# Plain copies of the weight-sum units on SyncE's queue, and units that begin at even and odd tiles in turn

## The chip, the core and the metric

The kernel runs on one core of a Trainium2 chip. The core has a matrix engine (PE, with its weight loads shown as PEld), a vector engine (DVE), a scalar engine (ACT), GpSimd (POOL) and SyncE (SP). Each engine works through its own instruction queue in order and waits for the others through semaphores. SP here only issues DMAs; POOL issues DMAs and also computes. The metric is the device time of one execution in microseconds, median over several runs; lower is better.

## What is computed

One transformer layer over 1024 tokens of width 1024. The part that matters here is the gated MLP:

```python
hn = rmsnorm(h, norm_ffn_g[i])
up = hn @ w_up[i]                       # 1024 x 5632
gt, val = up[..., :D_FF], up[..., D_FF:]
gt = causal_dwconv(gt, conv_w[i], conv_b[i])
h = h + (jax.nn.gelu(gt, approximate=False) * val) @ w_down[i]
```

Before it stand a pooling mixer and chunked attention with their projections, behind it a gated embedding and a last norm. D_FF is 2816.

## The kernel before

All matrix products are made in single precision from two halves of each number: every `mm3` is three matmuls (lines 130 to 132) of a high and a low part, and `split` (lines 134 to 136) makes the two parts, the high one on ACT (line 135) and the low one on DVE (line 136).

**The first projection** (called up here) goes over 22 tiles `fi` of 128 gate and 128 value columns. Each tile is a two by two block product made by seven products in place of eight, with sums and differences of the blocks (a scheme of Strassen's kind). A product is 12 matmuls, so a tile is 84. The order of the products in a tile is 1, 5, 2, 6, 3, 7, 4 (`steps`, line 710). Products 5, 6, 3 and 7 need sums of weight quarters. For tiles 3 to 21 POOL makes them (`summed`, line 758, the instruction of line 759) from quarters that SP loads (line 755) into a ring of buffers in the tiles F and X. What the products give is read out of PSUM by DVE and ACT: after product 6, DVE adds into `u2` (line 858), and product 7, which writes on into the same PSUM bank, cannot begin until DVE has done that. At the end of a tile come the convolution and the GELU (lines 869 to 882), the product of gate and value (lines 885 and 886) and the store of the tile to DRAM, `GD[fi]` (line 921, on SP).

**The second projection** (down) multiplies by `w_down`, with the same seven products over 11 pairs of tiles. Its weight sums are not made by POOL but by DMAs, ahead of time, in a DRAM array `SD`. There are 14 such units `u`: 0 to 2 belong to the first three tiles of up, 3 to 13 to `w_down`. `weight_sums(u, part)` (line 548) issues one of six parts. The even parts are plain copies (part 0: two copies of weights into `SD`; parts 2 and 4: one copy from `SD` to `SD` each). The odd parts are DMAs that add weights to what lies in `SD` (part 1: two of them; parts 3 and 5: one each). Every part reads what the part before it wrote. All of these transfers move 256 KB and are issued by POOL (line 556). Units 0 to 7 run during attention. Units 8 to 13 run during up, and only these are changed: 24 copies and 24 adding transfers.

In `up` (line 905) the units from 8 on are due by the tile's number: unit 8 + z begins at tile 5 + 2z and issues one part a tile, so that an odd tile issues only even parts (plain copies) and an even tile only odd parts (adding ones). Before them POOL does a small copy from the tile's GELU output (line 919), which ties the issue to that moment; `keep_in_program_order` pins an instruction behind the one traced before it on its engine.

**What sets the order.** PE's order is written out by hand. For the other engines a scheduler orders the instructions at build time by its own clock: an instruction that is not pinned can be moved ahead of others traced before it. The store of line 921 is not pinned, and loads of later tiles may go ahead of it. The launch sets a size for the scratch of dynamic DMAs (line 1261: `dynamic_dma_scratch_size=1024`).

## Time and profile before

| | us |
|---|---|
| median of 3 runs (lowest, highest) | 1145.69 (1145.26, 1145.73) |
| profiled execution, its own time | 1144.89 |
| its span, first to last instruction | 1143.1 |
| PE busy | 1124.2 |
| DVE busy | 887.3 |
| ACT busy | 577.8 |
| POOL busy | 292.1 |

The profile holds one execution. "Busy" is the time in which an engine has an instruction running. Matmuls overlap in the pipeline, so that a busy PE is not one at its peak. A row of the timeline has the start in us, the duration, the engine, the line of the kernel, the operation, what it writes and reads, and, where the engine stood idle before it, how long and which instruction seems to have released it. A row marked x3 merges three instructions. SPq rows are the issues on SP's queue. Stores of the tiles of up begin at 411.7 us (tile 0) and end at 812.8 us (tile 21).

### The profile page before, as it was taken

To read this page: it belongs to the slowest core of one execution; us is meant where nothing else is said; L and a number is where in the kernel's file an instruction comes from. 1 tells how busy PE (TensorE), PEld (TensorE's weight loads), DVE (VectorE), ACT (ScalarE), POOL (GpSimd) and SP (SyncE) were. 2 spreads that over 40 slices of the span, in tenths; PEclk is the share of its full clock that TensorE was granted. 3 is DMA by queue.
4 is the path that set the end of the run, shared out by engine and by line. 5 is a ranking of instruction groups with operands and counts; after the bars stand their busy time and mean duration, and the time that the engine had idled before them with its cause. 6 is when DMAs were issued, how large, how long until landed. Compare 5 with 4: busy or idle time off the path is not lost.

```text
span 1143.1 us, 15305 instructions
## 1 busy us (share of the span) xinstructions
PE 1124.2 (98%) x5517; PEld 945.0 (83%) x5517; DVE 887.3 (78%) x1371; ACT 577.8 (51%) x1001; POOL 292.1 (26%) x323
## 2 busy tenths in 40 slices
PE   8999999999999999999999999999999999999996
PEld 7988998888888878888887878788888888888886
DVE  7678878878756788989898888888896789757344
ACT  8568677765554543443433434343444557445222
POOL 0012324275002213445454645443000000000000
PEclk9999999999999999999999999999999999999998
DMA  7134656543500343133536463414683555310012
GB/s 265 38 86 113 160 122 172 120 90 131 185 10 19 120 158 100 65 120 92 147 104 173 97 171 101 102 37 127 229 280 98 169 186 176 108 48 1 1 74 75
DMA packets 62572, 133.46 MB, mean 117 GB/s; under 512 B 7392, under 2 KB 9696, under 8 KB 62048
## 3 DMA queue, kind: packets, MB, share of 16 engines
q1 hardware_dynamic: 49552, 100.96, 26.6%
q0 software_dynamic: 11200, 29.37, 12.9%
q10 hardware_dynamic: 1744, 2.17, 0.5%
q8 instruction: 43, 0.70, 0.3%
q14 instruction: 33, 0.27, 0.1%
HBM read 116.73 MB, written 45.09 MB: 142 GB/s over the span
## 4 chain that ended last, share of the span: by engine, by line
PE 84%; DVE 7%; ACT 3%; issue 3%; DMA 1%; POOL 1%; SPq 0%; DVEq 0%; POOLq 0%; ACTq 0%
PE PS L130 26%; PE PS L132 26%; PE PS L131 26%; PE PS L370 2%; DVE R L136 1%; PE PS L388 1%; ACT F L356 1%; PE PS L387 1%; DVE B L378 1%; POOL X L759 1%; DMA GD<-X 1%; DMA F<-in_w_qk 1%; DVE F L346 1%; DVE X L886 0%; PE PS L345 0%
## 5 line engine op out<-in xcount | busy, mean ns | idle before, releaser
L130 PE MATMUL PS<-R,R 128*128 128x512 f32 (+1 forms) x932 | 360.3, 387 | 5.9 <-DVE F L858 4.6
L132 PE MATMUL PS<-R,R 128*128 128x512 f32 (+1 forms) x932 | 356.3, 382 | 0.0
L131 PE MATMUL PS<-R,R 128*128 128x512 f32 x868 | 338.3, 390 | 0.4 <-DVE R L231 0.3
L130 PEld LDWEIGHTS PS<-R,R 128*128 128x128 f32 x932 | 175.5, 188 | 40.5 <-ACT R L135 7.0
L132 PEld LDWEIGHTS PS<-R,R 128*128 128x128 f32 x932 | 175.3, 188 | 34.4 <-DVE R L136 0.2
L131 PEld LDWEIGHTS PS<-R,R 128*128 128x128 f32 x868 | 163.5, 188 | 32.7 <-DVE R L231 1.4
L132 PE MATMUL PS<-B 128*128 128x512 f32 x316 | 123.1, 390 | 0.1
L130 PE MATMUL PS<-B 128*128 128x512 f32 x316 | 123.2, 390 | 0.0
L131 PE MATMUL PS<-B 128*128 128x512 f32 x316 | 123.0, 389 | 0.0
L136 DVE TENSOR_TENSOR R<-F,R 128x512 fp32r<-128x512 f32 (+1 forms) x117 | 93.9, 814 | 17.7 <-ACT R L135 17.3
L759 POOL TENSOR_TENSOR X<-X 128x512 f32<-128x512 f32 x42 | 77.3, 1840 | 116.5 <-DVE R L136 58.5
L135 ACT ACTIVATE R<-X 128x512 fp32r<-128x512 f32 x97 | 60.3, 629 | 88.2 <-PE PS L131 52.5
L136 DVE TENSOR_TENSOR R<-X,R 128x512 fp32r<-128x512 f32 x97 | 94.5, 975 | 12.2 <-ACT R L135 12.2
L135 ACT ACTIVATE R<-F 128x512 fp32r<-128x512 f32 (+1 forms) x121 | 71.9, 612 | 62.8 <-PE PS L131 26.3
L135 ACT ACTIVATE B<-F 128x512 fp32r<-128x512 f32 (+1 forms) x94 | 60.7, 647 | 78.2 <-PE PS L131 59.3
L659 POOL TENSOR_TENSOR small<-small 128x4 f32<-128x4 f32 (+1 forms) x7 | 8.1, 1161 | 336.2 <-DVE small L658 336.2
L136 DVE TENSOR_TENSOR B<-F,B 128x512 fp32r<-128x512 f32 (+1 forms) x94 | 66.4, 710 | 30.1 <-ACT B L135 30.0
L132 PEld LDWEIGHTS PS<-B 128*128 128x128 f32 x316 | 59.3, 188 | 12.9 <-DVE B L136 0.6
L131 PEld LDWEIGHTS PS<-B 128*128 128x128 f32 x316 | 59.3, 188 | 12.4
L130 PEld LDWEIGHTS PS<-B 128*128 128x128 f32 x316 | 59.3, 188 | 12.2
L131 PE MATMUL PS<-B,R 128*128 128x256 f32 (+1 forms) x208 | 64.0, 308 | 0.0
L356 ACT ACTIVATE F<-F,small 128x640 f32<-128x640 f32 (+2 forms) x64 | 44.4, 693 | 23.2 <-DVE small L354 15.7
(178 smaller groups left out, 2097.0 us busy)
## 6 DMA issues: line engine op xcount, KB each, us to landing
SD<-in_w_down POOLq DMA_DIRECT2D x66, 256.0 KB, 5.3
X<-in_w_up SPq DMA_DIRECT2D x53, 256.0 KB, 3.2
F<-SD SPq DMA_DIRECT2D x49, 256.0 KB, 2.7
R<-GD SPq DMA_DIRECT2D x44, 256.0 KB, 5.4
F<-in_w_down SPq DMA_DIRECT2D x33, 256.0 KB, 3.6
F<-in_w_up SPq DMA_DIRECT2D x32, 256.0 KB, 3.0
SD<-SD POOLq DMA_DIRECT2D x28, 256.0 KB, 3.8
GD<-X SPq DMA_DIRECT2D x11, 512.0 KB, 4.3
```

Source lines behind the costliest of these rows:

```text
L130: pe.matmul(ps, ahi, bhi, start=first, stop=False, skip_group_check=more)
L131: pe.matmul(ps, ahi, blo, start=False, stop=False, skip_group_check=more)
L132: pe.matmul(ps, alo, bhi, start=False, stop=last, skip_group_check=more)
L135: act.activation(hi, src, AF.Copy)
L136: dve.tensor_tensor(lo, src, rv(hi), ALU.subtract)
L346: dve.tensor_tensor_reduce(S.rearrange("p (a b) -> p a b", a=2), PS[:, 4:6, 0:320], b.rearrange("p (a b) -> p a b", a=2), 1.0, BIG, ALU.ad ...
L356: act.activation(S[:, 0:n], S[:, 0:n], AF.Exp, bias=s_[:, 0:1], scale=-1.0, accum_out=s_[:, 1:2])
L370: pe.transpose(pst[:, j * P:(j + 1) * P], S[:, j * P:(j + 1) * P], ident)
L378: dve.tensor_tensor(lo, pst, rv(hi), ALU.subtract)
L387: pe.matmul(O, V[:, k, h], pt[:, 0, idx], start=n_ == 0, stop=False)
L388: pe.matmul(O, V[:, k, h], pt[:, 1, idx], start=False, stop=n_ == len(ks) - 1)
L759: pool.tensor_tensor(rawu[to], rawu[a], rawu[b], op)
```

## The change

In `weight_sums` the engine that issues a plain copy becomes a parameter; its default is POOL, so that the units of the attention stage are as before. In `up` the plain copies go to SP, pinned behind the store of the tile, which itself is now pinned behind what was traced before it on SP. Adding transfers stay on POOL. A unit 8 + z now begins at tile 4 + 2z + (z mod 2): at tiles 4, 7, 8, 11, 12 and 15 where they were 5, 7, 9, 11, 13 and 15. So a tile now issues parts of both kinds. POOL's small copy of line 919 stands only in tiles where an adding part is due.

```diff
-        def weight_sums(u, part):
+        def weight_sums(u, part, copies=pool):
...
-                tc.keep_in_program_order(pool.dma_start(to, src, **({"accum_op": op} if op else {})))
+                tc.keep_in_program_order(pool.dma_start(to, src, accum_op=op) if op else copies.dma_start(to, src))
...
-            due = [(u, fi - 5 - 2 * (u - EARLY)) for u in range(EARLY, NK + UP_SUMS)
-                   if 0 <= fi - 5 - 2 * (u - EARLY) < 6]
-            if due:
+            due = [(EARLY + z, fi - 4 - 2 * z - z % 2) for z in range(NK + UP_SUMS - EARLY)]
+            due = [(u, part) for u, part in due if 0 <= part < 6]
+            if any(part % 2 for _, part in due):
                 tc.keep_in_program_order(pool.tensor_copy(small[:, 78:79], y[:, 0:1]))
             values_in(y)
-            sp.dma_start(GD[fi], y)
+            tc.keep_in_program_order(sp.dma_start(GD[fi], y))
             for u, part in due:
-                weight_sums(u, part)
+                weight_sums(u, part, sp)
```

## The prediction

> **What bounds the kernel now.** I read the page, then the waits of PE, then the stretch in which the changed transfers run, tile by tile, by the timelines of SP, POOL and DVE.

> ```profile
> span 1143.1 us, 15305 instructions
> PE 1124.2 (98%) x5517; PEld 945.0 (83%) x5517; DVE 887.3 (78%) x1371; ACT 577.8 (51%) x1001; POOL 292.1 (26%) x323
> ```

> PE is busy nearly all the time, so only gaps of PE can be won. The waits of PE between 480 and 830 us, where units 8 to 13 run, are one row:

> ```profile
> PE PS L130 <- DVE F L858: 3.8, 4, 1.2
> ```

> Four waits, all of product 7 for DVE's line 858. The same view on four short windows finds one each behind tiles 10, 14, 16 and 20; the row of the first (604 to 608 us):

> ```profile
> PE PS L130 <- DVE F L858: 1.0, 1, 1.0
> ```

> What they cost the whole is better read from the stores of the tiles (SP's timeline, with two rows of loads that I need below):

> ```profile
> 562.37 0.33 SPq L921 DMA_DIRECT2D GD<-X  x1
> ...
> 601.43 0.33 SPq L921 DMA_DIRECT2D GD<-X  x1
> ...
> 718.49 0.33 SPq L755 DMA_DIRECT2D F<-in_w_up  x1
> 737.07 0.33 SPq L921 DMA_DIRECT2D GD<-F  x1
> 756.11 0.33 SPq L921 DMA_DIRECT2D GD<-X  x1
> ...
> 778.04 1.53 SPq L755 DMA_DIRECT2D F<-in_w_up  x2
> ```

> Tile 17 is stored at 737.07, tile 18 at 756.11: an undisturbed tile takes 19.04 us. From tile 8 (562.37) to tile 17 there are nine: 171.36 us. They took 174.70. The excess, 3.34 us, holds the first three waits (behind tiles 10, 14 and 16) with the restart of PE after each. The fourth is behind tile 20.

> Now POOL around the store of tile 8 and of tile 10, and the held issues of tiles 12, 14 and 16:

> ```profile
> 558.61 2.54 POOL L556 DMA_DIRECT2D SD<-in_w_down  x3
> 561.36 2.15 POOL L759 TENSOR_TENSOR X<-X 128x512 f32<-128x512 f32 x1 [0.21 <-DVE R L136]
> ...
> 597.66 2.58 POOL L556 DMA_DIRECT2D SD<-in_w_down  x3
> 602.62 0.81 POOL L556 DMA_DIRECT2D SD<-in_w_down  x1 [2.38 <-DVE F L870]
> 603.17 1.57 POOL L759 TENSOR_TENSOR X<-X 128x512 f32<-128x512 f32 x1
> ...
> 636.02 2.57 POOL L556 DMA_DIRECT2D SD<-in_w_down  x3
> 640.72 0.81 POOL L556 DMA_DIRECT2D SD<-in_w_down  x1 [2.13 <-DVE R L136]
> ...
> 674.10 2.57 POOL L556 DMA_DIRECT2D SD<-in_w_down  x3
> 679.73 0.81 POOL L556 DMA_DIRECT2D SD<-in_w_down  x1 [3.06 <-DVE F L870]
> ...
> 714.12 2.54 POOL L556 DMA_DIRECT2D SD<-in_w_down  x3
> 718.93 0.81 POOL L556 DMA_DIRECT2D SD<-in_w_down  x1 [2.26 <-DVE R L136]
> ```

> Tile 8 issues three adding transfers, and the weight sum behind them (line 759, for product 7) runs at 561.36, 1.01 us ahead of the store. Tile 10 issues four. The first three go out, the fourth stands 2.38 us, and the sum comes at 603.17, 1.74 us behind the store: 2.75 us late. What held the fourth? The landing of the first of each group, from its own row (issues at 597.66, 636.02, 674.10, 714.12):

> ```profile
> DMA to landing us min/median/max: 4.6/4.6/4.6
> DMA to landing us min/median/max: 4.4/4.4/4.4
> DMA to landing us min/median/max: 5.3/5.3/5.3
> DMA to landing us min/median/max: 4.5/4.5/4.5
> ```

> The firsts land at 602.3, 640.4, 679.4 and 718.6. The fourths go at 602.62, 640.72, 679.73 and 718.93: 0.3 us behind the landing, four times of four. So three of these transfers fit in flight and the fourth waits for a place. The DVE instructions that the profile names ended at that moment by chance.

> The late sum then holds ACT, DVE and PE. DVE's rows of tiles 8 and 10:

> ```profile
> 565.17 0.68 DVE L858 TENSOR_TENSOR F<-PS,F 128x512 f32<-128x512 f32 x1
> ...
> 605.44 0.69 DVE L136 TENSOR_TENSOR R<-X,R 128x512 fp32r<-128x512 f32 x1 [2.83 <-ACT R L135]
> 606.05 0.68 DVE L858 TENSOR_TENSOR F<-PS,F 128x512 f32<-128x512 f32 x1
> ```

> DVE takes its queue in order: the split that needs the late sum (605.44) stands ahead of line 858. Undisturbed, line 858 ends 3.48 us behind the store (565.85 against 562.37); in tile 10 it ended 5.30 behind (606.73), and PE had waited 1.0 us, so it was wanted at 605.7. An undisturbed one would have ended at 601.43 + 3.48 = 604.9, with 0.8 us to spare. That is the small end of the slack, since tile 10's store was itself late: 39.06 us behind tile 8's, where two tiles are 38.08.

> **The change, part by part.** *The most adding transfers in one tile.* Before, tiles 10, 12, 14 and 16 have four each (parts 5 and 3 of one unit each and the two of part 1). With starts at 4, 7, 8, 11, 12, 15, the 24 adding transfers fall on tiles 5, 7 to 18 and 20, as 2, 1, 2, 3, 1, 1, 3, 3, 1, 1, 3, 1, 1 and 1. No tile has four; tiles 9, 12, 13 and 16 have three. Three is tile 8's case: all issued by 561.15, the sum not delayed, PE not waiting. So the holds go and the 3.34 us with them. Tiles 9 and 13 have their three at odd tiles, where only copies stood; no row shows three adding ones there, and tile 8's is the nearest.

> *What POOL no longer issues:* 24 copies. Tile 11 has four, of which these are the last two, with the sum behind them:

> ```profile
> 619.07 1.06 POOL L556 DMA_DIRECT2D SD<-in_w_down  x2
> 620.79 2.13 POOL L759 TENSOR_TENSOR F<-F 128x512 f32<-128x512 f32 x1 [0.66 <-DVE R L136]
> ```

> 0.53 us each, 12.7 us in all. POOL then stood 0.66 us for DVE, so the copies were covered and their removal is worth nothing. The two copies of line 919 that fall away (14 tiles in place of 16) are worth nothing for the same reason. [...]

> *What SP now issues:* up to three copies behind a store (tiles 8, 11, 12, 15). SP's issues take 0.33 us; at the 0.53 of POOL's as the upper bound three are 1.0 to 1.6 us. I take 0.33, the row of the same queue. Queued behind are the loads of line 755, which now wait for the pinned store and the copies. But between 718.49 and 778.04 SP issued no load of line 755 while three tiles ran: the loads are some three tiles ahead, and a few microseconds cost a product nothing. A copy waits for an adding transfer issued a tile earlier; the rows above show landings within 5.3 us, about a quarter of a tile, so there is no wait. An adding transfer in turn waits for copies issued behind the store before it, some 15 us earlier (19.04 less the 3.76 by which 558.61 stands ahead of tile 8's store).

> *The cover that could fail.* POOL makes product 5's sums ahead, as soon as a load lands:

> ```profile
> 569.43 1.46 POOL L759 TENSOR_TENSOR X<-X 128x512 f32<-128x512 f32 x1 [5.93 <-DMA X<-in_w_up]
> 573.13 3.97 POOL L759 TENSOR_TENSOR X<-X 128x512 f32<-128x512 f32 x2 [2.24 <-DVE R L136]
> ```

> This sum isn't urgent, but it stands in POOL's queue ahead of those of products 6 and 3. Between its end (570.89) and theirs (573.13) POOL has 2.24 us. Copies in front of the loads delay the landing: at 0.5 us each (the spacing of the issues in tile 11) by 1.5, at twice that by 3.1. Up to 2.24 us is free; the upper end pushes the urgent sums by 0.9, which just about uses up the 0.8 of slack. I take 0.1 us in all, nearest to the lower end, with 0 and 1 kept for the range. What a shifted sum does to DVE in tiles that go well I put at 0, with half a microsecond either way; in that lies the longest wait, 1.2 us behind tile 20, which has one adding transfer before and after.

> *The sum*, on the profiled execution's own 1144.89 (span 1143.1 and 1.8 around it): 1144.89 - 3.34 + 0.1 = 1141.65. The median of the runs lies 0.80 above that execution, so 1142.4. About 0.2% (2.3 us) is what a measurement of this kernel can tell from no change; 3.2 us is 0.28%.

> **Rivals.** *The holds stay (1145.7).* If a fourth transfer is held not for a place but by what DVE does at that moment, as the profile's releasers say, three in a tile are held too: four heavy tiles before, four after, and the 3.34 us stay. For it: the named releasers. Against it: tile 8's three and the 0.3 us. [...]

> *Half is given back (1144).* The sums made ahead shift by a microsecond or two and slow DVE in tiles that now go well, or the scheduler, whose clock sees other POOL and SP times, orders DVE less well. Two stalls of the size of those here (3.34 / 3 = 1.1 us) give 1142.4 + 2.2 = 1144.6; one gives 1143.5. I write 1144.

> *Slower (1148).* The loads fall so far behind the copies that the sum made ahead stands in the way of products 6 and 3 in every tile with three copies or three adding transfers: tiles 8, 9, 11, 12, 13, 15 and 16. It decides from a landing 3.0 us later than now (2.24 of room and 0.8 of slack). At 4.2 us later each tile loses 1.2: 7 x 1.2 = 8.4, and 1142.4 + 8.4 = 1150.8; with only the four tiles of three copies hit, 1147.2. I write 1148, between. Against it: it needs more than 1.4 us per copy, where tile 11's, issued 0.53 us apart, left the sum of line 759 on time.

> **Chances.** The forecast 0.62, the holds stay 0.12, half given back 0.17, slower 0.09. The forecast lies beyond 0.2% on the fast side, the two middle cases are within 0.2% (above 1143.4), the last is beyond it on the slow side: 0.62, 0.29, 0.09. The range goes from the forecast less 0.5 us and the spread of the runs (1.0 in all, 1141.4; I take 1141.2, since tile 20's wait may shrink too) up to the holds that stay, with the spread: 1146.2.

> **What would show it.** Right: no POOL row of line 556 with idle time of 2 us before it between 480 and 800 us; the sum behind the adding transfers about 1.0 us ahead of the store in every tile; PE's waits for line 858 down from four to one; stores of tiles 8 and 17 some 171.4 us apart; the loads of line 755 still ending around 718. Wrong: a held second or third adding transfer; PE waiting for another line of DVE; the sums of products 6 and 3 released by a load or by line 759 in the tiles with three copies; a longer wait behind tile 20.

## The result, and the profile after

| | before | after |
|---|---|---|
| runs of the first comparison: median (lowest to highest), us | 1145.47 (1143.16 to 1147.90) | 1139.30 (1138.51 to 1141.21) |
| profiled execution, us | 1144.89 | 1138.89 |
| its span, us | 1143.1 | 1137.1 |

The ratio after to before is 0.9953, with a 95% interval of 0.9938 to 0.9967. The change saved 6.2 us in this comparison where 3.2 were forecast, and the time lies below the low end of the range (1141.2). In all the comparisons of this study together the kernel before ran 77 times (one more run, at 4017 us, is left out): from 1141.93 to 1148.05, median 1144.72. The kernel after ran 17 times: median 1139.32, and fourteen of them lie between 1138.51 and 1139.66. By these the change is worth 5.4 us.

The page of the kernel after, the two rows shown of before:

```profile
span 1137.1 us, 15326 instructions
PE 1121.7 (99%) x5517; PEld 944.6 (83%) x5517; DVE 891.4 (78%) x1371; ACT 577.9 (51%) x1001; POOL 281.5 (25%) x297
```

PE has the same 5517 matmuls. Its busy time fell from 1124.2 to 1121.7, which idle time alone cannot do: some matmuls of before ran slower. This comes back below. The waits of PE between 475 and 825 us, one row as before (in total, times, longest):

```profile
PE PS L130 <- ACT R L135: 1.4, 1, 1.4
```

Of the four waits for line 858 none is left. The one wait that remains is behind tile 20, as before, now for ACT's split. Next SP's timeline at the stores of tiles 8 and 17:

```profile
560.58 0.33 SPq L921 DMA_DIRECT2D GD<-X  x1
561.00 0.48 SPq L556 DMA_DIRECT2D SD<-SD  x1
561.53 1.31 SPq L556 DMA_DIRECT2D SD<-in_w_down  x2
562.94 2.07 SPq L755 DMA_DIRECT2D X<-in_w_up  x3
...
731.65 0.33 SPq L921 DMA_DIRECT2D GD<-F  x1
```

From tile 8 to tile 17 it is 171.07 us where it was 174.70, and where nine undisturbed tiles are 171.36. The three copies now stand between the store and the loads, and the first load goes out 2.36 us behind the store (562.94 - 560.58). POOL's timeline in tiles 9 and 12, two of the four with three adding transfers:

```profile
576.32 2.50 POOL L556 DMA_DIRECT2D SD<-in_w_down  x3
579.07 2.14 POOL L759 TENSOR_TENSOR X<-X 128x512 f32<-128x512 f32 x1 [0.25 <-DVE R L136]
...
633.68 2.52 POOL L556 DMA_DIRECT2D SD<-in_w_down  x3
636.43 2.14 POOL L759 TENSOR_TENSOR X<-X 128x512 f32<-128x512 f32 x1 [0.23 <-DVE R L136]
```

All three go out without a hold and the sum follows them within 0.3 us, where it came 2.9 us behind the third in tile 10 of before. So the forecast's four signs are there: no held row of line 556, the sum ahead of the store (1.0 us in most tiles, but only 0.17 in tile 13, where POOL's chain is late and PE still doesn't wait), no wait for line 858, and the stores 171.1 us apart. Lined up matmul by matmul, the kernel after gains 1.27, 0.94 and 1.11 us at the three waits, 3.3 in all. But it has gained 2.0 us already in the first 15 us, where the two programs are the same. The remaining 0.7 of the 6.0 us between the two executions lies behind the store of the last tile and was not followed up. The same two windows of before and then of after (us, busy time of PE, PEld, DVE, ACT, POOL, the granted clock, DMA share, GB/s):

```profile
0.00:10.00 10.00, 7.36 (x21) 4.76 (x21) 3.51 (x9) 5.05 (x8) 0.74 (x7) 1.00 0.79 244
10.00:15.00 5.00, 4.49 (x12) 3.32 (x13) 4.71 (x8) 4.97 (x10) 0.00 (x0) 0.66 1.02 372
```

```profile
0.00:10.00 10.00, 7.70 (x22) 5.07 (x22) 3.88 (x10) 5.61 (x9) 0.73 (x7) 1.00 0.78 251
10.00:15.00 5.00, 4.71 (x25) 3.85 (x25) 4.86 (x8) 4.92 (x10) 0.00 (x0) 1.00 1.04 401
```

Before made 12 matmuls between 10 and 15 us at a mean granted clock of 0.66, after 25 at 1.00. Two questions follow. Is the hold really a matter of room, and which part of the change removes it? And where does the rest of the gain come from, the holds or the start?

### The profile page after: what moved, and what is told of

The parts are those of the page before. It is cut to its first block, busy times and chain, and to the rows that moved or that the text cites. A ratio compares the mean times of both kernels' runs of the same rounds, so it can differ in the third digit from the quotient of the medians.

```text
span 1137.1 us, 15326 instructions
## 1 busy us (share of the span) xinstructions
PE 1121.7 (99%) x5517; PEld 944.6 (83%) x5517; DVE 891.4 (78%) x1371; ACT 577.9 (51%) x1001; POOL 281.5 (25%) x297
## 4 chain that ended last, share of the span: by engine, by line
PE 88%; DVE 6%; ACT 2%; issue 2%; DMA 1%; SPq 0%; DVEq 0%; POOLq 0%; POOL 0%; ACTq 0%
PE PS L130 27%; PE PS L132 27%; PE PS L131 27%; PE PS L370 2%; PE PS L387 1%; PE PS L388 1%; DVE R L136 1%; DVE B L378 1%; ACT F L356 1%; PE PS L344 1%; PE PS L345 1%; DMA F<-in_w_qk 0%; DVE F L346 0%; DMA R<-GD 0%; PE PS L353 0%
## 5 line engine op out<-in xcount | busy, mean ns | idle before, releaser
L130 PE MATMUL PS<-R,R 128*128 128x512 f32 (+1 forms) x932 | 359.7, 386 | 2.7 <-ACT R L135 1.4
L130 PEld LDWEIGHTS PS<-R,R 128*128 128x128 f32 x932 | 175.2, 188 | 35.5 <-ACT R L135 3.1
L130 PE MATMUL PS<-B 128*128 128x512 f32 x316 | 123.3, 390 | 0.0
L759 POOL TENSOR_TENSOR X<-X 128x512 f32<-128x512 f32 x42 | 80.2, 1912 | 122.9 <-DVE R L136 71.2
L136 DVE TENSOR_TENSOR R<-F,R 128x512 fp32r<-128x512 f32 (+1 forms) x117 | 94.0, 815 | 19.9 <-ACT R L135 19.4
L135 ACT ACTIVATE R<-F 128x512 fp32r<-128x512 f32 (+1 forms) x121 | 72.2, 613 | 72.1 <-PE PS L131 31.1
L135 ACT ACTIVATE R<-X 128x512 fp32r<-128x512 f32 x97 | 60.6, 629 | 86.0 <-PE PS L131 58.1
L136 DVE TENSOR_TENSOR R<-X,R 128x512 fp32r<-128x512 f32 x97 | 97.3, 1004 | 0.6 <-ACT R L135 0.6
L135 ACT ACTIVATE B<-F 128x512 fp32r<-128x512 f32 (+1 forms) x94 | 60.6, 646 | 70.6 <-PE PS L131 54.4
L136 DVE TENSOR_TENSOR B<-F,B 128x512 fp32r<-128x512 f32 (+1 forms) x94 | 66.6, 712 | 26.2 <-ACT B L135 25.9
L130 PEld LDWEIGHTS PS<-B 128*128 128x128 f32 x316 | 59.4, 188 | 12.1
L759 POOL TENSOR_TENSOR F<-F 128x512 f32<-128x512 f32 x20 | 38.0, 1900 | 75.0 <-DVE R L136 34.9
```

The costliest lines, as they stand in the source:

```text
L130: pe.matmul(ps, ahi, bhi, start=first, stop=False, skip_group_check=more)
L135: act.activation(hi, src, AF.Copy)
L136: dve.tensor_tensor(lo, src, rv(hi), ALU.subtract)
L759: pool.tensor_tensor(rawu[to], rawu[a], rawu[b], op)
```

## The experiments

Theory A: the fourth adding transfer waits for room in the scratch of POOL's DMAs, and the holds are the whole gain; the start is luck. Rivals: the hold is made by what DVE does, as the profile's releasers say; the move to SP is what gains; the change makes the start faster (theory B).

**The kernel after once more.** No edit.

> The changed kernel again, five rounds beside the kernel before. In the two profiles the stretch from the store of tile 8 to that of tile 17 went from 174.70 us to 171.07 (560.58 to 731.65), and another 2.0 us of the difference arose in the first 15 us, where before shows a granted clock of 0.66 between 10 and 15 us and after shows 1.00. Theory A (the holds make about 3.3 us, the start is luck): the start differs from run to run in both kernels, and runs of equal granted clock differ by 3.3 to 4 us (ratio 0.9965 to 0.9972). Theory B (the change makes the start too): all runs of after have the better start, none of before, and the difference is 5.3 us or more (ratio below 0.9955).

Measured: 1139.32 us (1138.87 to 1141.75), ratio 0.9946 (0.9934 to 0.9957). The gain is as large as the first time. By the number theory A missed (it wanted 0.9965 or more), and theory B's ratio came out; but theory B also wanted the better start in every run of after, and one of the six (1141.75 us, mean granted clock 0.995 where the others have 0.997) is some 2 us longer than the rest. Which one holds is left to the runs with a quiet start, further down.

**Room alone.** The kernel before with one number changed:

```diff
-    nc = bacc.Bacc("TRN2", target_bir_lowering=False, num_devices=1, dynamic_dma_scratch_size=1024)
+    nc = bacc.Bacc("TRN2", target_bir_lowering=False, num_devices=1, dynamic_dma_scratch_size=1536)
```

> The kernel before with one number changed: the scratch of dynamic DMAs 1536 in place of 1024. All transfers stay on POOL, starts as before. Theory A (the fourth adding transfer of tiles 10, 12, 14 and 16 waits for room in that scratch): no idle time of 2 us ahead of a fourth one, the stretch from tile 8 to tile 17 falls from 174.7 to about 171.4 us, the kernel is 3.3 us faster. Rival 1 (the fourth is held by what DVE does at that moment): the four holds of 2.1 to 3.1 us stay, the stretch stays at 174.7, no gain. Rival 2 (taking the copies off POOL makes the gain): no gain either.

Measured: 1139.53 us (1139.07 to 1142.37), ratio 0.9948 (0.9936 to 0.9960), where the kernel after took 1139.32 in the same comparison: all but 0.2 us of the gain, with no transfer moved. POOL's timeline in tile 10, which still has four adding transfers:

```profile
596.00 3.38 POOL L556 DMA_DIRECT2D SD<-in_w_down  x4
599.04 1.85 POOL L759 TENSOR_TENSOR X<-X 128x512 f32<-128x512 f32 x1
```

The four go out in one run of 3.38 us, where the fourth of before stood 2.38 us. Two rivals fall with this: DVE's work is the same as before, so it is not DVE that held the fourth, and the gain needs no move.

**Less room.** The opposite dose, on the kernel after: the same number at 768.

> The kernel after with a smaller scratch for dynamic DMAs (768 in place of 1024). Theory A (room in the scratch decides, three adding transfers fit into 1024, so two fit into 768): in tiles 9, 12, 13 and 16 the third adding transfer now stands until the first has landed, the sum behind it comes late again, and the time goes back to about that of the kernel before: 1143 to 1148 us. Rival (not room but the number of four, or what DVE does at that moment): no hold at a third transfer, 1139.3 us within 1.

Measured: 1145.11 us (1144.02 to 1148.42), ratio 1.0007 (0.9995 to 1.0019): the gain is gone. POOL in tile 9:

```profile
576.48 1.67 POOL L556 DMA_DIRECT2D SD<-in_w_down  x2
581.69 0.81 POOL L556 DMA_DIRECT2D SD<-in_w_down  x1 [3.54 <-DVE F L870]
582.24 1.57 POOL L759 TENSOR_TENSOR X<-X 128x512 f32<-128x512 f32 x1
```

and the landing of the first of the group, issued at 576.48:

```profile
DMA to landing us min/median/max: 4.9/4.9/4.9
```

Now the third is held. It goes at 581.69, 0.3 us behind the landing of the first (576.48 + 4.9 = 581.4), the same rule as before at another count. Two adding transfers fit into 768, three into 1024, four at least into 1536. Room decides; the count follows it.

**The move alone.** Copies on SP behind the store as in the change, units still beginning at tiles 5, 7, 9, 11, 13 and 15, scratch 1024 (the main lines; the pinned store and the condition of POOL's small copy are as in the change too):

```diff
-                tc.keep_in_program_order(pool.dma_start(to, src, **({"accum_op": op} if op else {})))
+                tc.keep_in_program_order(pool.dma_start(to, src, accum_op=op) if op else copies.dma_start(to, src))
...
-                weight_sums(u, part)
+                weight_sums(u, part, sp)
```

> One half of the change: plain copies on SP behind the pinned stores, but the units begin at tiles 5, 7, 9, 11, 13, 15 as before, so that tiles 10, 12, 14 and 16 still have four adding transfers. Theory A: the four holds and the excess of 3.3 us stay, PE waits three times for line 858 as before, the time is that of before within 1 us. Rival (the move makes the gain): PE's waits go and it is 3 us or more faster.

Measured: 1150.11 us (1147.51 to 1152.21), ratio 1.0041 (1.0028 to 1.0054). That is a miss: the move alone is no neutral act, it is 4.5 us slower. POOL's timeline around tile 10, first before, then the move alone:

```profile
587.96 1.36 POOL L759 TENSOR_TENSOR X<-X 128x512 f32<-128x512 f32 x1 [5.43 <-DMA X<-in_w_up]
593.15 2.28 POOL L759 TENSOR_TENSOR X<-X 128x512 f32<-128x512 f32 x1 [3.83 <-DVE R L136]
595.50 1.63 POOL L759 TENSOR_TENSOR X<-X,F 128x512 f32<-128x512 f32 x1
597.08 0.65 POOL L919 COPY small<-X 128x1 f32<-128x1 f32 x1
```

```profile
590.44 3.95 POOL L759 TENSOR_TENSOR X<-X 128x512 f32<-128x512 f32 x2 [9.00 <-DVE R L136]
594.47 1.62 POOL L759 TENSOR_TENSOR X<-X,F 128x512 f32<-128x512 f32 x1
596.03 1.18 POOL L919 COPY small<-X 128x1 f32<-128x1 f32 x1
597.15 2.50 POOL L556 DMA_DIRECT2D SD<-in_w_down  x3
602.12 0.80 POOL L556 DMA_DIRECT2D SD<-in_w_down  x1 [2.46 <-issue]
```

Before, the sum made ahead stands alone at 587.96, and POOL idles 3.83 us before the urgent ones. With four copies ahead of them on SP the first of the three loads goes out 2.98 us behind the store of tile 9 in place of 1.70, and the loads take 6.3 us to land in the median in place of 3.5. In both runs the sum made ahead begins 0.16 us behind the landing of the second load (587.80 and 590.28), so that it seems to be the landing that lets it go, though the row names DVE. It begins at 590.44 and runs straight into the urgent sum (x2, without a gap), and all that follows on POOL is late, the adding transfers too. PE at the wait, before and then the move alone:

```profile
605.50 0.39 PE L132 MATMUL PS<-R,R 128*128 128x512 f32 x1
606.88 0.47 PE L130 MATMUL PS<-R,R 128*128 128x512 f32 x1 [0.99 <-DVE F L858]
607.18 0.39 PE L131 MATMUL PS<-R,R 128*128 128x512 f32 x1
```

```profile
603.75 0.39 PE L132 MATMUL PS<-R,R 128*128 128x512 f32 x1
606.36 0.47 PE L130 MATMUL PS<-R,R 128*128 128x512 f32 x1 [2.23 <-DVE F L858]
606.67 0.40 PE L131 MATMUL PS<-R,R 128*128 128x512 f32 x1
606.91 0.57 PE L132 MATMUL PS<-R,R 128*128 128x512 f32 x1
607.27 0.63 PE L130 MATMUL PS<-R,R 128*128 128x512 f32 x1
607.70 0.63 PE L131 MATMUL PS<-R,R 128*128 128x512 f32 x1
```

Seen from the last matmul ahead of the wait, the group of adding transfers went out 7.84 us earlier before (605.50 - 597.66) and 6.60 us earlier here (603.75 - 597.15). It is 1.24 us later, and the wait is 1.24 us longer: 2.23 against 0.99. And the longer wait has a second price: the matmuls behind it start 0.43 us apart instead of 0.23, for 3.41 us by the clock record of the trace. Lined up matmul by matmul this costs another 1.5 us.

**The move with room.** The same kernel with a scratch of 1536.

> The copies on SyncE with the old starts at tiles 5, 7, 9 and so on, which took 1150.1 us, now with a scratch of 1536 in place of 1024. Theory A (the move costs only through the holds that stay: the loads behind the copies shift the sums made ahead, so that PE stands longer at a held sum): without holds the move is worth nothing, 1139.5 us within 0.7. Rival (copies ahead of the loads cost time by themselves): above 1141.5 us, with waits of PE in tiles 9 to 17 that have no held transfer before them.

Measured: 1140.96 us (1139.75 to 1142.0), ratio 0.9967 (0.9955 to 0.9978), between the two expectations. Most of the harm went with the holds. It lies 1.4 us above the 1139.53 of room without the move, but that was timed in another comparison, so the two were run once more side by side.

> The kernel before with a scratch of 1536, again, as the measure for the run with the copies on SyncE and the same scratch, which was timed in another comparison. Both theories: 1139.5 us within 0.5.

> The same with the copies on SyncE and the old starts. Theory (copies ahead of the loads cost by themselves, since the sums made ahead run into the urgent ones): 1.0 to 1.8 us above the run ahead of it, about 1140.9 us. Rival (the 1.4 us of the first time came from comparing two sessions): within 0.5 us of it.

Measured: 1140.30 us (1138.78 to 1140.94) with room alone, 1141.07 (1140.23 to 1142.99) with the copies on SP as well: 0.8 us, less than the theory asked and more than the rival. Room alone missed its expectation, 1139.5 within 0.5. In this comparison before took 1144.40 and the kernel after 1139.58 (below), so that room alone gave 4.1 of 4.8 us. The holds don't make that difference: from the store of tile 0 to that of tile 17 the two profiles have 322.10 and 322.26 us. The ratios to before, 0.9963 (0.9951 to 0.9975) and 0.9974 (0.9965 to 0.9984), overlap too, so the profiles have to decide. In the one with room alone PE waits for nothing between 475 and 740 us; with the move there are two waits for line 858:

```profile
PE PS L130 <- DVE F L858: 0.6, 2, 0.3
```

Matmul by matmul the move loses 0.5 us behind tile 12 and 0.5 behind tile 16. POOL in tile 12 of the first of the two runs with the move:

```profile
630.22 1.33 POOL L759 TENSOR_TENSOR F<-F 128x512 f32<-128x512 f32 x1 [10.08 <-DMA F<-in_w_up]
631.51 3.97 POOL L759 TENSOR_TENSOR X<-X 128x512 f32<-128x512 f32 x2
635.42 0.65 POOL L919 COPY small<-X 128x1 f32<-128x1 f32 x1
636.01 3.34 POOL L556 DMA_DIRECT2D SD<-in_w_down  x4
638.17 2.96 POOL L759 TENSOR_TENSOR X<-X 128x512 f32<-128x512 f32 x1
```

No transfer is held, yet the sum for product 7 begins at 638.17, 0.81 us behind the store (637.36): POOL had waited 10.08 us for a load and then had no gap left. So the copies ahead of the loads cost some 0.8 us by themselves.

**The new starts alone.** The new due tiles, all transfers on POOL (its small copy of line 919 in every due tile, the store pinned as in the change):

```diff
-            due = [(u, fi - 5 - 2 * (u - EARLY)) for u in range(EARLY, NK + UP_SUMS)
-                   if 0 <= fi - 5 - 2 * (u - EARLY) < 6]
+            due = [(EARLY + z, fi - 4 - 2 * z - z % 2) for z in range(NK + UP_SUMS - EARLY)]
+            due = [(u, part) for u, part in due if 0 <= part < 6]
```

> The other half: units begin at tiles 4, 7, 8, 11, 12, 15, but the copies stay on POOL behind its small copy of line 919, so that tile 12 issues three adding transfers and three copies from POOL, tiles 8, 9, 13, 15 and 16 four or five transfers. Theory A, with room counted by size and adding transfers larger than copies: at most one or two holds (tile 12 first), two thirds or more of the gain, 2.2 to 3.3 us faster than before. Rival 1 (room counted in transfers, four at most less one): holds in tiles 8, 9, 12, 13, 15 and 16, no gain or slower by up to 3 us. Rival 2 (the move makes the gain): no gain.

Measured: 1139.82 us (1139.46 to 1143.47), ratio 0.9954 (0.9940 to 0.9967): nearly all of the gain. One hold is left, in tile 12, where three adding transfers and three copies come together:

```profile
634.70 2.54 POOL L556 DMA_DIRECT2D SD<-in_w_down  x3
639.11 0.55 POOL L556 DMA_DIRECT2D SD<-in_w_down  x1 [1.87 <-DVE F L870]
639.67 1.30 POOL L759 TENSOR_TENSOR X<-X 128x512 f32<-128x512 f32 x1
```

The held one is a copy, the sixth of the group (two had gone at 633.64 and 634.21). So copies take room as well, but less than adding transfers: five with two copies among them fit where four adding ones do not. PE waited 1.2 us for line 858 there. What the move adds to the new starts is 0.5 us (1139.82 to 1139.32), inside the intervals.

**Before, two more profiles.** No edit, one execution each.

> The kernel before once more, unchanged, for a second profile of it. Theory A (the holds cost more in most executions than in the first profile, and a long enough wait of PE behind one is followed by matmuls at half the granted clock): the time between the stores of tiles 8 and 17 is above 174.7 us, up to 178, with matmuls 0.43 us apart for some 3 us behind the longest wait; the start then has no slow stretch or one of 2 us. Theory B (the holds cost the 3.34 us of the first profile in every execution, and the rest of the gain is the start): tile 8 to 17 takes 174.7 us within 0.3, and the first 15 us are about 2 us longer than in the kernel after.

> The same kernel as the run ahead of it, for a third profile. Theory A: again above 174.7 us between the stores of tiles 8 and 17, and not the same number as in the others, since the holds end with a landing whose time differs between executions. Theory B: 174.7 us within 0.3.

The two took 1144.14 and 1147.34 us. Stores of tiles 8 and 17 of the first, then of the second:

```profile
560.55 0.33 SPq L921 DMA_DIRECT2D GD<-X  x1
...
736.50 0.33 SPq L921 DMA_DIRECT2D GD<-F  x1
```

```profile
562.64 0.33 SPq L921 DMA_DIRECT2D GD<-X  x1
...
739.31 0.33 SPq L921 DMA_DIRECT2D GD<-F  x1
```

175.95 and 176.67 us, where the profile of the prediction had 174.70: the holds cost 4.6 and 5.3 us beyond 171.36, not 3.34. PE waits three times in this stretch again, but behind tiles 10, 12 and 14, where it had waited behind 10, 14 and 16. Matmul by matmul against the kernel after the three cost 2.0, 1.4 and 1.2 us in the one and 1.6, 2.1 and 1.6 in the other. In tile 10 of the first of these runs the fourth transfer stood 3.13 us, where it had stood 2.38. The first has no slow stretch at its start, the second has one of 2 us. Theory A holds for the holds' size; its second half does not: neither profile shows matmuls at half the clock behind a hold (behind the longest wait, 1.85 us in the second of them, the granted clock is 1.00 between 648 and 652 us). Only the move alone showed that.

The traces show two things that set the size of such a wait: when the first transfer of the group lands (4.2 to 5.5 us behind its issue), and how early the group goes out. Counted from PE's last matmul ahead of the place of the wait, it goes either 7.8 or 8.8 us earlier in the four profiles with before's transfers and room (these three, and the one with two more matmuls further down). DVE's line 861, the last product ahead of the convolution, goes with it. In the first profile, tiles 10 and 12:

```profile
588.09 1.78 DVE L861 TENSOR_TENSOR F<-F 128x512 f32<-128x512 f32 x1
...
627.43 0.69 DVE L861 TENSOR_TENSOR F<-F 128x512 f32<-128x512 f32 x1
627.92 1.36 POOL L759 TENSOR_TENSOR F<-F 128x512 f32<-128x512 f32 x1 [4.99 <-DMA F<-in_w_up]
```

In tile 10 POOL's sum made ahead was already running (587.96, shown above) and line 861 took 1.78 us; in tile 12 it began behind DVE, and the line took 0.69. It is so in all 16 groups of the four profiles: eight times 1.78 and 7.8 us, eight times 0.68 or 0.69 and 8.8. The profiles have two, two, three and one of the late groups, and the holds cost 3.3, 4.6, 5.3 and 2.6 us. So the landing of a load, which releases the sum made ahead, has a part in the price too. This is read from the traces; no run changed it alone.

**The start taken out.** Two more matmuls on a constant behind the first 12 of the first product, where PE stands 0.5 to 1.6 us for ACT, in the kernel after and in the kernel before:

```diff
+FILLERS = {0: 2}
...
             if k < KT - 1:
                 start_mm(k)
+            for _ in range(FILLERS.get(k, 0)):
+                pe.matmul(PS[:, 7], warm[:, 0:P], warm, start=True, stop=True)
```

> The kernel after, with two more matmuls on a constant behind the first 12 of the first product, where PE stands 0.55 to 1.25 us for ACT. Theory (the slow stretch of the start, 3.41 us at half the granted clock, comes where this wait is 1.2 us long, in one run out of six): the median stays at 1139.3 us within 0.3, and no run lies 2 us above it. Rival (the stretch doesn't come from this wait): single runs at 1141 to 1143 us remain.

> The kernel before with the same two matmuls. Theory A (the gain is the holds, the start is the same luck in both kernels): the median falls by less than 0.8 us, to 1144 to 1145, and runs still differ by 3 us or more, since the holds do. Theory B (the start costs before about 2 us in most runs, and after not): the median falls by 2 us or more.

Measured: after with it 1139.20 us (1138.70 to 1140.35; 6 runs), before with it 1143.91 (1141.82 to 1145.28; 12 runs), in a comparison in which before took 1144.72 (1143.25 to 1147.78). The ratio of before with it to before is 0.9987 (0.9977 to 0.9997). So the start makes up 0.8 us of the level of before (0.3 to 2.6 by the interval), at the edge of what theory A allowed, and next to nothing of the median of after, of which 3 of 17 runs are some 2 us longer than the rest. Runs whose mean granted clock is 0.995 or lower, as in the first profile of before, are about as frequent in both kernels: 13 of the 71 runs of before with a clock on record, 3 of 17 of after. (A rough count: the third profile of before has a slow start at 0.996.) Theory B, a slow start in most runs of before and in none of after, falls with this. With the start quiet in both, the gap is 1143.91 - 1139.20 = 4.7 us. In the profile of before with the two matmuls the three waits cost 0.4, 0.7 and 1.6 us, matmul by matmul: one more size of the same holds.

**The last wait.** Tile 20's gated output goes to the other buffer of the pair, in the kernel after, so that what is written into the place it had need not wait for its store to land:

```diff
+        def y_of(fi):
+            return Yb if fi == NF - 2 else Ys[fi % 2]
+
-            y = Ys[fi % 2][:, ts]
+            y = y_of(fi)[:, ts]
...
-            y = Ys[fi % 2]
+            y = y_of(fi)
```

> The kernel after, with the gated output of tile 20 written to the other buffer of the pair, so that ACT's high half of the first factor of the second projection, which takes that place, needn't wait for the store of tile 20 to land. Theory (the wait of 1.4 us that PE has left behind tile 20 is that landing): the wait goes, and the time falls to 1138.0 us, between 1137.6 and 1138.6. Rival (something else of the step into the second projection is late right behind it): the wait only changes its name, 1139.3 us within 0.4.

Measured: 1138.41 us (1137.86 to 1140.0), ratio 0.9940 (0.9927 to 0.9954). PE's waits between 785 and 825 us:

```profile
PE PS L131 <- DVE B L136: 0.5, 1, 0.5
```

The wait of 1.4 us behind tile 20 became one of 0.5 under another name, and the median is 0.9 below the 1139.32 of all runs of the kernel after.

**Both edits on the kernel after.**

> The kernel after with both edits that were tried on it alone: tile 20's gated output in the other buffer (1138.4 us alone) and two more matmuls at the start (1139.2 us alone). Theory (the two are at opposite ends of the kernel and don't meet): 1138.3 us, between 1137.8 and 1138.8, and no run above 1140. Rival (the order that the scheduler finds with both is worse than with one): above 1138.8 us.

Measured: 1137.90 us (1137.01 to 1138.12), ratio 0.9946 (0.9933 to 0.9960) against a before of 1144.04 in that comparison. In its profile the view of PE's waits has no row between 475 and 825 us. Since before was quick in that comparison, this kernel and the kernel after were timed side by side.

> The kernel after, as the measure for the next. 1139.3 us within 0.4.

> The kernel after with tile 20's output in the other buffer and the two matmuls at the start. Theory (its 1137.9 us was a gain over the kernel after): 1.0 to 1.6 us below the run ahead of it. Rival (the session was a fast one for every kernel, as before's 1144.0 there suggests): within 0.5 us of it.

Measured: after 1139.58 us (1138.85 to 1141.74), with both edits 1137.96 (1137.68 to 1138.59), before 1144.40. It is 1.6 us under the kernel after and the fastest version of this study.

## Why the prediction had the right mechanism and the wrong size

*The holds are a matter of room, three in flight.* Right, and shown from both sides: 1536 lets four through, 768 holds the third, and the held one goes 0.3 us behind the landing of its group's first transfer, in 25 holds of 25 in the seven profiles that have any.

*No tile has four, so the three waits go.* Right: 171.07 us from tile 8 to tile 17, where 171.4 was named as the sign.

*"So the holds go and the 3.34 us with them."* This is the step that failed, by its size. For the execution from which it was read 3.34 us is right. But it was set against the median of the runs as if it were the same in each, and it isn't: four profiles of kernels with these holds show 3.3, 4.6, 5.3 and 2.6 us. It hangs on the landing of the first transfer (4.2 to 5.5 us) and on how early the group goes out (7.8 or 8.8 us ahead of PE's last matmul before the wait), and both differ. With room alone the runs gained 6.1 and 4.1 us in two comparisons, and with the start quiet the medians are 4.7 apart. What makes a landing early or late from run to run was not tried.

*"The sum, on the profiled execution's own 1144.89."* This base held 2.0 us of a slow start that the forecast did not see, since it looked at PE's waits between 480 and 830 us and not at the clock of each stretch. The profiled execution was rather low in holds and high at its start, and so came out 0.8 us from the median as if it were a typical one. That 0.8 was then added to the kernel after as well, though holds larger than 3.34 us, which lift the median of before, are gone there. So the miss of 3.1 us (1142.4 forecast, 1139.3 measured) is 2.0 of slow start, 0.8 of this step and 0.1 of the term for the cover, for which PE showed no wait; 0.2 are left over. The medians divide the gain into 0.8 us for the start and 4.7 for the rest, mostly holds; they are differences of the same three medians, so that their sum of 5.5 is no proof against the 5.4 of all runs. The comparisons with the kernel after in them had 6.2, 6.3 and 4.8, as the median of before lay at 1145.47, 1145.62 and 1144.40.

*The range.* "The spread of the runs" stood in it with half a microsecond, read off three runs of before that agreed by chance within 0.47 us. 77 runs spread over 6.1. Three close runs do not bound a time that hangs on landings.

*The move is worth nothing.* Right on top of the new starts (0.5 us, inside the intervals), wrong as a general term: with the old starts it costs 4.5 us while the holds stay and about 0.8 us without them. The zero came from POOL's side, its 0.66 us of waiting behind the copies of tile 11. The runs show SP's: the copies stand ahead of loads there, these go out later and take longer to land (2.98 us behind the store in place of 1.70, and 6.3 us in place of 3.5, in tile 9 of the move alone), and POOL's sum for such a load stands ahead of the urgent ones.

*The cover that could fail* was therefore the right place to look, and its 2.24 us of room was real: in the kernel after it holds, narrowly in tile 13, and in the move alone it does not. The "slower" rival is the mechanism of that run. The old starts put four copies in front of a tile's loads, the new ones at most three; that this is why the change escapes was not tested by itself.

*The holds stay* and *half is given back*: both refuted, by the profile of after and by the scratch of 1536. That a shifted sum slows DVE, as the second of them said, is seen in the kernel before itself, in line 861 (1.78 us in place of 0.69); the forecast put it at 0, with half a microsecond either way.

## What to carry to other kernels

When a queue stands and a landing ends the stand, try the size of what it waits for first: here one number, the scratch, gave what a new schedule of the transfers gave. Price a wait that ends with a DMA's landing from several executions, and put its spread into the range; one profile is one draw. Read the clock of every stretch of the profile, the first microseconds too, before its total is taken as the base of a sum.

## What the runs showed of the hardware that was not expected

In these runs the size of the scratch for dynamic DMAs set how many of POOL's adding transfers of 256 KB went out without a hold: two at 768, three at 1024, four, the most that a tile has, at 1536. The next issue went 0.3 us behind the landing of the first. POOL's whole queue stood meanwhile, its arithmetic too: in tile 10 of before the fourth transfer stood 2.38 us, and the sum came behind it at 603.17.

```profile
605.00:607.50 2.50, 1.14 (x4) 0.98 (x5) 2.50 (x5) 0.93 (x2) 0.00 (x0) 0.89 1.11 249
607.50:611.00 3.50, 3.50 (x10) 2.74 (x10) 1.14 (x3) 1.24 (x1) 1.05 (x1) 0.59 0.51 156
```

Nine matmuls start in 3.5 us, at a mean granted clock of 0.59. The record of the clock has one stretch at 0.5 here, from 606.96 us on for 3.413 us; it begins 0.6 us behind the end of the wait. In the start of before a wait of 1.24 us, which ended at 10.22 us, was followed by such a stretch from 11.26 us on, 3.413 us long as well. In the third profile one of 1.25 us was followed by matmuls 0.43 us apart from 12.46 us on, at a granted clock of 0.76 between 10 and 17 us. A wait of 1.06 us at the same place (second profile) was not followed by one: the matmuls behind it start 0.23 us apart. Neither were the longest waits behind the holds: 1.74 us in the second profile, where three waits of 3.8 us in all cost 4.6, and 1.85 us in the third, with the clock of 1.00 given above. The length of the wait alone does not decide it.

In the records of before and after, the stretches of one clock that end within the execution last 6.827 us (1.0), 3.413 (0.5) and 1119.572 (1.0) in before and 1126.397 (1.0) in after: 2, 1, 328 and 330 times 3.4133 us. What decides whether a wait is followed by a slow stretch stays open.
